# Eight closing stages: the last four k rows of the first 512 columns move next to the second 512 columns, token tile by token tile

## The chip, the cores and the metric

The kernel runs on one core of a Trainium2 chip. The metric is device time in microseconds (us). A core has engines that run their own instruction streams side by side and wait for one another through semaphores: PE (TensorE, matmuls and transposes through the identity matrix), DVE (VectorE), ACT (ScalarE), POOL (GpSimd), and SP, which issues the DMAs here. Each engine takes its instructions in the order in which the build has put them: an instruction that waits holds back everything behind it on its engine.

## What is computed

512 tokens of 1024 features go through four layers. Layer 1 has a state-space mixer (S5 with a GLU), layer 2 a latent attention (MLA), layers 3 and 4 a sparse attention (DSA) beside a gating branch. Each mixer is followed by a feed-forward block. Every one of the eight sub-blocks ends in the same way, and this is all that the change touches:

```python
# y: 512 x K, K = 1024 (out projections) or the last rows of a feed-forward
h = layer_norm(ALPHA * h + y @ w_out, g, b)      # w_out: K x 1024
def layer_norm(x, g, b):
    mu  = mean(x, -1); var = mean(square(x - mu), -1)
    return (x - mu) * rsqrt(var + 1e-5) * g + b
```

Layers 3 and 4 add a gated per-layer embedding, `(p @ w_ple) * sigmoid(x @ w_ple_gate)`, to the feed-forward's sum, and x there is the result of the out projection's LayerNorm.

## The kernel before

Everything is float32. A product is split into three matmuls: the high part `hi` (an ACT cast, L249, in `wpiece`) and the rest `lo` (a subtraction, L109, on DVE or on POOL while the counter `lo_pool`, set to LP = 10, lasts) of the weights, and `xh`, `xl` of the data. `mm3` issues them as L265, L266, L267. A weight piece is two k rows (2 x 128 x 512); raw weights come by SP's DMAs (L242).

**A closing stage.** The eight stages, in the order of time with the moment T (us from the start of the span) at which the last matmul of the stage ends: 1 `ssm_w_out` (328.2), 2 `w_ff2` of layer 1 (673.3), 3 `attn_w_o` (894.7), 4 `w_ff2` of layer 2 (1237.1), 5 `w_o` of layer 3 (1465.6), 6 `w_ffn_out` of layer 3 (1870.0), 7 `w_o` of layer 4 (2097.3), 8 `w_ffn_out` of layer 4 (2515.3). Stages 1, 3, 5, 7 are written in `proj_ln`, stages 2, 4, 6, 8 in `plain`. Tokens lie in four tiles t0 to t3 of 128, each with two PSUM banks: the first 512 columns (nh 0) and the second (nh 1).

`tm_gen` (L280) runs nh 0 weight piece by weight piece over all four token tiles and evacuates the four banks at its end (the residual sum and, later, a LayerNorm statistic; DVE). In stages 3, 5 and 7 these matmuls are fillers of the attention's last units (`proj_first`, L1145). For nh 1 the argument `stagger` is set: all weight pieces are prepared first, then token tile after token tile takes its 24 matmuls (18 in stages 6 and 8), its evacuation and `close` (L422): the rest of the LayerNorm, some 20 DVE instructions, four of them on 128 x 512 elements (L119, two with the mean `mv`, two with the inverse deviation `vy`).

The finished tile is put on `pending`. `flush` (L447) takes one from there and turns it to feature-major with eight transposes on PE (`to_fm`, L127), and the casts and subtractions (`xh` on ACT, `xl` on DVE) that the next stage reads. In `tm_gen` a flush follows a token tile where more than two tiles are pending (L331). So the PE's program has, at the end of a stage: t2's matmuls, to_fm of t0, t3's matmuls, to_fm of t1, then the first matmuls of the next stage, with to_fm of t2 and of t3 among them. Stage 8 has no transposes; it writes the output.

**What sets the order.** A scheduler in the build places all instructions of the program on their engines by an estimate of times, so the order on an engine can differ from the order in which the code is written. What it places doesn't change at run time. Tiles named in the rows carry running numbers.

## Time and profile before

| | before |
|---|---|
| time, median of 3 runs | 2529.29 us (2528.91 to 2530.14) |
| the profiled execution's own time | 2529.88 us |
| span of that execution | 2528.1 us |
| PE busy | 2411.3 us (95%), 11961 matmuls |
| DVE busy | 1559.1 us (62%) |
| ACT busy | 968.8 us (38%) |
| POOL busy | 389.0 us (15%) |
| PE's waits for a LayerNorm's result ahead of a transpose (L127 behind DVE x L119) | 30.8 us in 10 waits |
| mean granted TensorE clock | 0.973 of full speed |

The span counts from the first to the last recorded instruction; 1.8 us of the execution's time lie around it. A timeline row reads: start in us, duration in us, engine, line, operation, output tile <- input tiles, shapes, how many in a row (x), and in brackets the idle time of the engine just before it with the instruction that ended it. The duration of a row "x2" is that of both together. Matmuls overlap, so the pitch of two rows is what one takes.

### The profile page before, as it was taken

What the parts mean: (1) busy time and instruction counts of PE and PEld (TensorE: products, weight loads), DVE (VectorE), ACT (ScalarE), POOL (GpSimd) and SP (SyncE); (2) the same over time, 40 slices, a digit from 0 to 9 for tenths busy, and PEclk for the clock granted to TensorE, in tenths of its full rate; (3) what the DMA queues carried; (4) which work ended last, traced back from release to release, by engine and by line L of the source; (5) the groups of instructions that cost most, each with busy time, mean ns of one, the idle gap of its engine ahead of it and who ended that gap; (6) DMA issues with size and microseconds to landing.
All of it is one profiled execution on the core that took longest, in us unless ns stands there. A gap on an engine that the chain in (4) does not pass through costs nothing.

```text
span 2528.1 us, 30717 instructions
## 1 busy us (share of the span) xinstructions
PE 2411.3 (95%) x11961; PEld 1988.5 (79%) x11961; DVE 1559.1 (62%) x2898; ACT 968.8 (38%) x1563; POOL 389.0 (15%) x378
## 2 busy tenths in 40 slices
PE   7799999999989999999999999999989998999997
PEld 6667888888877888888776878888877687888886
DVE  8744366765666567765695573555569556355655
ACT  4213235445245335444246432333324643223331
POOL 1100110000231220000246220000034622000001
PEclk9779999999999999999999999999999999999999
DMA  4224243322221533222232235232123123423211
GB/s 110 57 57 133 84 150 101 98 88 81 85 71 51 167 92 109 92 92 67 78 127 51 84 121 179 67 133 67 60 86 127 51 86 107 167 67 117 84 59 59
DMA packets 182897, 237.55 MB, mean 94 GB/s; under 512 B 19728, under 2 KB 118816, under 8 KB 182688
## 3 DMA queue, kind: packets, MB, share of 16 engines
q1 hardware_dynamic: 182752, 235.59, 29.5%
q8 instruction: 94, 1.54, 0.3%
q14 instruction: 51, 0.42, 0.1%
HBM read 224.56 MB, written 11.01 MB: 93 GB/s over the span
## 4 chain that ended last, share of the span: by engine, by line
PE 82%; DVE 15%; ACT 2%; DMA 1%; issue 1%; SPq 0%; DVEq 0%; POOL 0%; ACTq 0%
PE ps L265 26%; PE ps L266 25%; PE ps L267 25%; PE ps L127 3%; DVE x L119 2%; PE ps L791 2%; DVE sc L1451 2%; DVE m L1450 2%; DVE x L109 1%; PE ps L789 1%; PE ps L459 1%; DVE vy L109 1%; DVE xl L109 1%; DVE ab L109 1%; DVE sc L119 1%
## 5 line engine op out<-in xcount | busy, mean ns | idle before, releaser
L109 POOL TENSOR_TENSOR wl<-wr,wh 128x1024 fp32r<-128x1024 f32 (+4 forms) x124 | 278.2, 2253 | 1810.9 <-ACT wh L249 1127.0
L249 ACT CAST wh<-wr 128x1024 fp32r<-128x1024 f32 (+4 forms) x300 | 305.7, 1021 | 578.8 <-PE ps L266 287.4
L267 PE MATMUL ps<-xh,wl 128*128 128x512 f32 x1248 | 485.9, 390 | 4.3 <-DVE wl L109 4.3
L265 PE MATMUL ps<-xh,wh 128*128 128x512 f32 x1248 | 486.2, 390 | 0.0
L266 PE MATMUL ps<-xl,wh 128*128 128x512 f32 x1248 | 486.2, 390 | 0.0
L109 DVE TENSOR_TENSOR wl<-wr,wh 128x1024 fp32r<-128x1024 f32 x176 | 217.2, 1236 | 226.5 <-ACT wh L249 225.4
L109 DVE TENSOR_TENSOR wl<-wq,wh 128x1024 fp32r<-128x1024 f32 x140 | 170.5, 1221 | 178.1 <-ACT wh L249 177.7
L267 PEld LDWEIGHTS ps<-xh,wl 128*128 128x128 f32 x1248 | 234.7, 188 | 53.4 <-DVE wl L109 4.7
L265 PE MATMUL ps<-wh,xh 128*128 128x512 f32 (+4 forms) x704 | 270.9, 386 | 4.5 <-DVE rp L109 2.0
L266 PEld LDWEIGHTS ps<-xl,wh 128*128 128x128 f32 x1248 | 234.8, 188 | 48.8
L265 PEld LDWEIGHTS ps<-xh,wh 128*128 128x128 f32 x1248 | 234.6, 188 | 48.6
L266 PE MATMUL ps<-wl,xh 128*128 128x512 f32 (+4 forms) x704 | 263.6, 375 | 0.0
L267 PE MATMUL ps<-wh,xl 128*128 128x512 f32 (+4 forms) x704 | 262.6, 376 | 0.5 <-DVE xl L109 0.5
L249 ACT CAST wh<-wq 128x1024 fp32r<-128x1024 f32 x140 | 147.3, 1052 | 284.1 <-PE ps L266 234.5
L266 PE MATMUL ps<-wl,sh 128*128 128x512 f32 x560 | 217.8, 389 | 0.0
L267 PE MATMUL ps<-wh,sl 128*128 128x512 f32 x560 | 217.5, 389 | 0.0
L265 PE MATMUL ps<-wh,sh 128*128 128x512 f32 x560 | 216.9, 389 | 0.0
L265 PEld LDWEIGHTS ps<-wh,xh 128*128 128x128 f32 x704 | 136.9, 195 | 31.4 <-ACT xh L122 3.5
L267 PEld LDWEIGHTS ps<-wh,xl 128*128 128x128 f32 x704 | 136.1, 194 | 22.1 <-DVE xl L109 1.1
L266 PEld LDWEIGHTS ps<-wl,xh 128*128 128x128 f32 x704 | 137.0, 195 | 18.5
L109 DVE TENSOR_TENSOR x<-x,ps 128x512 f32<-128x512 f32 x156 | 103.0, 681 | 73.4 <-PE ps L267 73.1
L127 PE MATMUL ps<-ident,x 128*128 128x128 f32 x576 | 97.6, 289 | 47.3 <-DVE x L119 30.8
(368 smaller groups left out, 3910.8 us busy)
## 6 DMA issues: line engine op xcount, KB each, us to landing
wr<-in_w_ffn_in_dram SPq DMA_DIRECT2D x44, 1024.0 KB, 5.1
wr<-in_w_ff_dram SPq DMA_DIRECT2D x40, 1024.0 KB, 5.5
wq<-in_w_ff_dram SPq DMA_DIRECT2D x24, 1024.0 KB, 5.1
wq<-in_w_ffn_out_dram SPq DMA_DIRECT2D x16, 1024.0 KB, 8.2
wr<-in_w_in_dram SPq DMA_DIRECT2D x12, 1024.0 KB, 5.5
wr<-in_w_ple_gate_dram SPq DMA_DIRECT2D x8, 1024.0 KB, 5.1
wr<-in_ssm_w_glu_dram SPq DMA_DIRECT2D x6, 1024.0 KB, 5.6
xs<-x SPq DMA_DIRECT2D x24, 256.0 KB, 2.0
```

The source lines that it names most:

```text
L109: (eng or self.nc.vector).tensor_tensor(out, a, b, op)
L119: (eng or self.nc.vector).scalar_tensor_tensor(out, a, s, b, op0, op1)
L127: self.nc.tensor.transpose(out, in_, self.ident[:k, :k])
L249: self.nc.scalar.copy(hi, src)
L265: mm(ps, lh, rh, start=first, stop=False)
L266: mm(ps, lh, rl, start=False, stop=False)
L267: mm(ps, ll, rh, start=False, stop=last)
L459: self.nc.tensor.matmul(bk[:, c], w[:, kt], self.Xh(kt)[:, c], start=kt == 0 and w is hi, stop=False)
L789: nc.tensor.matmul(o, u[:, q * 8 + j, sl], T[:, m * 2 + h, jj], start=True, stop=False)
L791: nc.tensor.matmul(o, H[sl, r, j], ca[sl, r, j].rearrange("p d c -> p (d c)"), start=False, stop=r == 1)
L1450: self.nc.vector.max(m8, s)
L1451: self.nc.vector.match_replace(s, m8, s, -3e38)
```

## The change

The new helpers `begin` and `finish` take the place of both passes. `begin` runs nh 0 with all k rows but the last four, piece by piece over the four token tiles. `finish` prepares the pieces of those last four rows (`p0`) and all pieces of nh 1 (`p1`), and then takes token tile after token tile: 12 matmuls for the rest of nh 0, its evacuation, 24 (18) matmuls of nh 1, its evacuation and `close`. A flush follows where more than one tile is pending, before it was more than two. `p0` gets buffers of its own: in `proj_ln` from a new pool "tail", in `plain` from the tags `sh` and `sl` of the stage's pool. The counter LP = 10 for POOL is set ahead of `p0`. The loads of g and b (`gb`) come later on SP. `proj_first` no longer evacuates, and in stages 5 and 7 no longer splits its pieces over finer steps than `begin` does.

```diff
-    def wpiece(self, src):
+    def wpiece(self, src, spare=None):
         a, b = src.shape[1:]
-        hi = self.tile(self.wp, [P, a, b], F32R, "wh", 5)
-        lo = self.tile(self.wp, [P, a, b], F32R, "wl", 5)
+        if spare is None:
+            hi = self.tile(self.wp, [P, a, b], F32R, "wh", 5)
+            lo = self.tile(self.wp, [P, a, b], F32R, "wl", 5)
+        else:
+            hi, lo = (self.tile(spare, [P, a, b], F32R, tag, 2) for tag in ("sh", "sl"))
...
+    def begin(self, wsrc, xh, xl, order, acc):
+        m = len(order) - 4
+        for pc, ks in self.pieces(wsrc(0), order[:m]):
+            for t in range(NT):
+                if len(acc) <= t:
+                    acc.append(self.bank())
+                self.times(acc[t], t, pc, ks, xh, xl, ks[0] == order[0], False)
+                yield
+
+    def finish(self, wsrc, xh, xl, order, gb, acc, final=None, spare=None):
+        m = len(order) - 4
         gb = self.gb(*gb)
+        if final is None:
+            self.fm_ln()
+        ev0, ev1 = self.residual(False)(0), self.close_ln(gb, 1, False, final)
+        self.lo_pool = LP
+        p0 = list(self.pieces(wsrc(0), order[m:], spare))
+        p1 = list(self.pieces(wsrc(1), order))
+        for t in range(NT):
+            for pc, ks in p0:
+                self.times(acc[t], t, pc, ks, xh, xl, False, ks[-1] == order[-1])
+            ev0(t, acc[t])
+            bk = self.bank()
+            for pc, ks in p1:
+                self.times(bk, t, pc, ks, xh, xl, ks[0] == order[0], ks[-1] == order[-1])
+            ev1(t, bk)
+            if len(self.pending) > 1:
+                self.flush()
...
-        self.fm_ln()
-        for nh in range(2):
-            ev = self.close_ln(gb, nh, True) if nh else self.residual(True)(nh)
-            if nh == 0 and first is not None:
-                for _ in first:
-                    pass
-                continue
-            self.tm(wsrc(nh), list(order), 512, xh, xl, ev, stagger=nh == 1)
...
+        for _ in first:
+            pass
+        if self.X is None:
+            self.unspill()
+        with self.phase("tail") as pool:
+            self.finish(wsrc, xh, xl, order, gb, acc, spare=pool)
```

The lines of the matmuls move by three (L265 to L268 and so on), L249 to L252, L360 to L363. The number and shapes of matmuls, DVE operations and DMAs stay.

Where the instructions stand on PE at the end of stage 5, before. `ps2183` is the bank of nh 1 of t2, `ps2193` that of t3, x2149 and x2150 the two halves of t0, x2151 and x2152 those of t1; `ps2214` belongs to the next stage.

```order
L267 MATMUL ps2183_12085<-wh2165_11981,xl2047_11412 128x512
L127 MATMUL ps2191_12135<-ident2_68,x2149_11944 128x128 x4
L127 MATMUL ps2192_12142<-ident2_68,x2150_11945 128x128 x4
L265 MATMUL ps2193_12149<-wh2158_11966,xh2046_11411 128x512
...
L267 MATMUL ps2193_12149<-wh2165_11981,xl2047_11412 128x512
L127 MATMUL ps2201_12199<-ident2_68,x2151_11946 128x128 x4
L127 MATMUL ps2202_12206<-ident2_68,x2152_11947 128x128 x4
L265 MATMUL ps2214_12236<-wh2205_12218,xh2142_11883 128x512
```

The transposes of t0 stand behind t2's matmuls, those of t1 behind t3's, and the next stage follows.

The same place on PE in the change. `ps2102` is the bank of nh 0 of t3, `ps2185` nh 1 of t2, `ps2195` nh 1 of t3; x2138 and x2139 are t0, x2140 and x2141 t1, x2142 and x2143 t2. Nh 1 of t0 and t1 and the rest of nh 0 of all four tiles stand ahead of the first row.

```order
L270 MATMUL ps2102_11658<-sh2155_11919,xl2047_11420 128x512
L127 MATMUL ps2183_12070<-ident2_68,x2138_11883 128x128 x4
L127 MATMUL ps2184_12077<-ident2_68,x2139_11884 128x128 x4
L268 MATMUL ps2185_12097<-wh2158_11925,xh2046_11419 128x512
...
L127 MATMUL ps2193_12147<-ident2_68,x2140_11885 128x128 x4
L127 MATMUL ps2194_12154<-ident2_68,x2141_11886 128x128 x4
L268 MATMUL ps2195_12174<-wh2158_11925,xh2046_11419 128x512
...
L127 MATMUL ps2203_12224<-ident2_68,x2142_11887 128x128 x4
L127 MATMUL ps2204_12231<-ident2_68,x2143_11888 128x128 x4
L268 MATMUL ps2216_12262<-wh2207_12244,xh2150_11910 128x512
```

Each tile's transposes have moved forward by one token tile: t0's stand directly behind the last matmul of nh 0, t2's directly behind the last matmul of the stage.

DVE at that place in the change: from the evacuation of `ps2102` to the end of t0's LayerNorm.

```order
L119 SCALAR_TENSOR_TENSOR x2144_11889<-x2144_11889,ps2102_11658 128x512
...
L119 SCALAR_TENSOR_TENSOR x2140_11885<-x2140_11885,mv2176_12046,x2146_11902 128x512
L119 SCALAR_TENSOR_TENSOR x2141_11886<-x2141_11886,mv2176_12046,x2147_11904 128x512
L363 BN_STATS st2197_12201<-x2144_11889 128x6
L114 TENSOR_SCALAR rs12180_12054<-ve2178_12051 128x1
L116 TENSOR_SCALAR rt12173_11992<-vy2171_11989,ve2170_11988 128x1
...
L109 TENSOR_TENSOR vy2171_11989<-vy2171_11989,rq12174_11993 128x1
L116 TENSOR_SCALAR rq12182_12056<-rq12182_12056,rt12181_12055 128x1
L119 SCALAR_TENSOR_TENSOR x2138_11883<-x2138_11883,vy2171_11989,x2148_11906 128x512
L119 SCALAR_TENSOR_TENSOR x2139_11884<-x2139_11884,vy2171_11989,x2149_11908 128x512
```

The evacuation of t3 now stands ahead of the last step of t0's LayerNorm, with 21 instructions between the first row and the last two. Stage 7 has the same order with other numbers.

DVE at the end of stage 1 in the change: x296 and x297 are t2, `ps424` is nh 1 of t3, the last matmuls of the stage.

```order
L116 TENSOR_SCALAR rq1421_2481<-rq1421_2481,rt1420_2480 128x1
L119 SCALAR_TENSOR_TENSOR x299_1766<-x299_1766,ps424_2522 128x512
L109 TENSOR_TENSOR vy418_2477<-vy418_2477,rq1421_2481 128x1
L363 BN_STATS st426_2549<-x299_1766 128x6
L119 SCALAR_TENSOR_TENSOR x296_1760<-x296_1760,vy418_2477,x377_2256 128x512
L119 SCALAR_TENSOR_TENSOR x297_1762<-x297_1762,vy418_2477,x378_2258 128x512
```

The last two steps of t2's LayerNorm stand behind the evacuation of t3, and t2's transposes are the ones that now follow the stage's last matmul on PE. Stages 2, 4 and 6 have this order too, stage 6 with more instructions between.

## Rows read from the trace of the kernel before

**Rows 1.** The page: busy time of each engine; shares of the chain that ended last.

```profile
PE 2411.3 (95%) x11961; PEld 1988.5 (79%) x11961; DVE 1559.1 (62%) x2898; ACT 968.8 (38%) x1563; POOL 389.0 (15%) x378
...
PE 82%; DVE 15%; ACT 2%; DMA 1%; issue 1%; SPq 0%; DVEq 0%; POOL 0%; ACTq 0%
```

**Rows 2.** Waits of PE: line waited for: us in total, times, longest.

```profile
PE ps L127 <- DVE x L119: 30.8, 10, 5.5
```

**Rows 3.** Timeline of PE around T in stages 1 to 7 (columns as above).

```profile
327.78 0.39 PE L267 MATMUL ps<-wh,h 128*128 128x512 f32 x1
333.63 1.97 PE L127 MATMUL ps<-ident,x 128*128 128x128 f32 x8 [5.47 <-DVE x L119]
...
676.42 0.90 PE L127 MATMUL ps<-ident,x 128*128 128x128 f32 x3 [3.15 <-DVE x L119]
...
897.52 1.11 PE L127 MATMUL ps<-ident,x 128*128 128x128 f32 x4 [2.10 <-DVE x L119]
...
906.84 0.33 PE L127 MATMUL ps<-ident,x 128*128 128x128 f32 x1 [0.72 <-DVE vy L116]
...
1240.35 0.66 PE L127 MATMUL ps<-ident,x 128*128 128x128 f32 x4 [3.21 <-DVE x L119]
...
1470.35 1.77 PE L127 MATMUL ps<-ident,x 128*128 128x128 f32 x8 [4.71 <-DVE x L119]
...
1864.56 1.32 PE L127 MATMUL ps<-ident,x 128*128 128x128 f32 x8 [1.44 <-DVE x L119]
...
1872.34 0.66 PE L127 MATMUL ps<-ident,x 128*128 128x128 f32 x4 [2.35 <-DVE x L119]
...
2101.98 1.85 PE L127 MATMUL ps<-ident,x 128*128 128x128 f32 x8 [4.71 <-DVE x L119]
...
2106.91 1.54 PE L127 MATMUL ps<-ident,a 128*128 128x128 f32 x6 [2.65 <-DMA a<-in_p_dram]
```

**Rows 4.** Timeline of DVE in stage 1, of POOL in stages 1 and 5.

```profile
328.52 2.22 DVE L109 TENSOR_TENSOR vy<-vy,rq 128x1 f32<-128x1 f32 x1
...
330.78 3.46 DVE L119 SCALAR_TENSOR_TENSOR x<-x,vy,x 128x512 f32<-128x512 f32 x2
...
325.29 7.74 POOL L109 TENSOR_TENSOR wl<-wr,wh 128x1024 fp32r<-128x1024 f32 x3 [16.21 <-ACT wh L249]
...
1462.73 7.02 POOL L109 TENSOR_TENSOR wl<-wr,wh 128x1024 fp32r<-128x1024 f32 x3 [6.64 <-ACT wh L249]
```

**Rows 5.** Timeline of PE and DVE behind the last matmul of stage 8.

```profile
2514.92 0.39 PE L267 MATMUL ps<-wh,wq 128*128 128x512 f32 x1
...
2515.75 0.68 DVE L109 TENSOR_TENSOR x<-x,ps 128x512 f32<-128x512 f32 x1
...
2517.49 1.36 DVE L119 SCALAR_TENSOR_TENSOR x<-x,vy,x 128x512 f32<-128x512 f32 x2
...
2518.89 1.41 DVE L119 SCALAR_TENSOR_TENSOR x<-x,mv,x 128x512 f32<-128x512 f32 x2
...
2520.22 0.15 DVE L109 TENSOR_TENSOR vy<-vy,rt 128x1 f32<-128x1 f32 x1
...
2521.40 1.42 DVE L119 SCALAR_TENSOR_TENSOR x<-x,vy,x 128x512 f32<-128x512 f32 x2
...
2523.67 1.41 DVE L119 SCALAR_TENSOR_TENSOR x<-x,vy,x 128x512 f32<-128x512 f32 x2
```

**Rows 6.** Windows: length, busy time of each engine (instructions), granted clock, DMA share, GB/s.

```profile
1425.00:1446.00 21.00, 21.00 (x124) 17.71 (x123) 10.25 (x24) 8.00 (x19) 5.94 (x12) 1.00 0.68 227
1470.00:1475.00 5.00, 4.65 (x17) 3.79 (x18) 5.00 (x13) 3.40 (x4) 1.23 (x1) 0.66 0.60 210
2105.00:2110.00 5.00, 3.09 (x11) 2.52 (x12) 5.00 (x11) 1.63 (x5) 2.35 (x1) 0.50 0.44 154
```

More of the change, by code (lines that the diff above doesn't have):

```diff
@@ L1030, in plain @@
     def plain(self, pool, n, H, w, row, gb, final):
-        gb = self.gb(*gb)
-        if final is None:
-            self.fm_ln()
         parts = []
@@ L1041, in plain @@
         pick = lambda i: (lambda k: Cols(*(parts[k // n * 2 + t][:, i, k % n] for t in range(2))))
-        for nh in range(2):
-            ev = self.close_ln(gb, nh, False, final) if nh else self.residual(False)(nh)
-            self.tm(self.wslab(w, nh * 512, 512, row), list(range(2 * n)), 512, pick(0), pick(1), ev, stagger=nh == 1)
+        wsrc = lambda nh: self.wslab(w, nh * 512, 512, row)
+        order, acc = list(range(2 * n)), []
+        for _ in self.begin(wsrc, pick(0), pick(1), order, acc):
+            pass
+        self.finish(wsrc, pick(0), pick(1), order, gb, acc, final, pool)
     def strassen(self, pool, n, H, w, row):
@@ L1128, in strassen, with pieces, times @@
         yield
-    def proj_ln(self, wsrc, xh, xl, gb, order=tuple(range(8)), first=None):
-        gb = self.gb(*gb)
+    def pieces(self, wsrc, kts, spare=None):
+        for i in range(0, len(kts), 4):
+            g = kts[i:i + 4]
+            raw = self.wraw(wsrc(g), len(g), 512)
+            for j in range(0, len(g), 2):
+                m = min(2, len(g) - j)
+                yield self.wpiece(raw[:, j:j + m], spare), g[j:j + m]
+    def times(self, bank, t, piece, ks, xh, xl, first, last):
+        hi, lo = piece
+        for i, k in enumerate(ks):
+            self.mm3(bank, xh(k)[:, t * P:(t + 1) * P], xl(k)[:, t * P:(t + 1) * P], hi[:, i], lo[:, i],
+                     first and i == 0, last and i == len(ks) - 1)
@@ L1132, in proj_ln @@
+    def proj_ln(self, wsrc, xh, xl, gb, order=tuple(range(8)), first=None, acc=None):
+        order = list(order)
         if first is None:
             self.new_r()
-        self.fm_ln()
-        for nh in range(2):
-            ev = self.close_ln(gb, nh, True) if nh else self.residual(True)(nh)
-            if nh == 0 and first is not None:
-                for _ in first:
-                    pass
-                continue
-            self.tm(wsrc(nh), list(order), 512, xh, xl, ev, stagger=nh == 1)
@@ L1143, in proj_first @@
-    def proj_first(self, wsrc, xh, xl, order=tuple(range(8)), fine=False):
-        self.new_r()
-        def evac(t, ps):
-            if self.X is None:
-                self.unspill()
-            self.residual(True)(0)(t, ps)
-        return self.tm_gen(wsrc(0), list(order), 512, xh, xl, evac, fine=fine)
+            acc = []
+            first = self.begin(wsrc, xh, xl, order, acc)
+        for _ in first:
+            pass
+        if self.X is None:
+            self.unspill()
+        with self.phase("tail") as pool:
+            self.finish(wsrc, xh, xl, order, gb, acc, spare=pool)
@@ L1153, in rope, with proj_first @@
+    def proj_first(self, wsrc, xh, xl, order=tuple(range(8))):
+        self.new_r()
+        acc = []
+        return self.begin(wsrc, xh, xl, list(order), acc), acc
     def rope(self, dst, src, half, t, c0):
@@ L1406, in mla_ @@
         pick = lambda x: (lambda k: x[:, k])
-        first = self.proj_first(wsrc, pick(oh), pick(ol))
+        first, acc = self.proj_first(wsrc, pick(oh), pick(ol))
         self.attend(units, 2, [(len(units), first)])
-        return lambda: self.proj_ln(wsrc, pick(oh), pick(ol), gb, first=first)
+        return lambda: self.proj_ln(wsrc, pick(oh), pick(ol), gb, first=first, acc=acc)
     def sgu_prep(self, sgu_w, sgu_b):
@@ L1651, in dsa_ @@
             order = list(range(4, 8)) + list(range(4))
-            first = self.proj_first(wsrc, pick("h"), pick("l"), order, True)
+            first, acc = self.proj_first(wsrc, pick("h"), pick("l"), order)
             def some(gen, n):
@@ L1660, in dsa_ @@
                                      (len(units) + 2, first)])
-        return lambda: self.proj_ln(wsrc, pick("h"), pick("l"), gb, order, first=first)
+        return lambda: self.proj_ln(wsrc, pick("h"), pick("l"), gb, order, first=first, acc=acc)
     def swiglu(self, p, w_in, w_out, w_ple, w_pg, gb, final):
```

## The prediction

> **What bounds the kernel now.** I read the page first: PE is busy 95% of the span, and the chain that ended last is PE for 82% and DVE for 15% [rows 1]. So a closing stage costs what PE computes there, which the change leaves alone, plus what PE waits there. Second, PE's waits: the transposes of finished token tiles wait for the LayerNorm's last step in ten places, 30.8 us together [rows 2]. Third, the timeline of PE around T [rows 3]: the largest of these waits begins at T in every stage. In stage 1 the last matmul begins at 327.78, and to_fm of t1 begins at 333.63 after 5.47 us of idle time. The others are 3.15 (stage 2), 2.10 with 0.72 behind it (3), 3.21 (4), 4.71 (5), 1.44 and 2.35 (6), 4.71 (7); stage 7 has 2.65 more for a transfer of p. Fourth, DVE and POOL at that time [rows 4]: POOL subtracts the next stage's lo pieces, 7.74 us in three operations from 325.29, and in these stretches DVE operations that read two SBUF tensors stretch: a `vy` multiplication on 128 x 1 elements takes 2.22 us and a pair of the last LayerNorm step 3.46, where such a pair takes 1.42 and a small operation 0.15 at the end of stage 8 [rows 5]. POOL starts when t3's matmuls free weight buffers, 2.9 us before T in stages 1 and 5 [rows 3, 4], and t3 stays last in the change, so I leave these stretches where they are.
>
> The Trainium skill, GPSIMD Engine Reference, section 1 Specifications, says that POOL and DVE share their SBUF interfaces and contend where a DVE instruction has two SBUF inputs. The rows agree with that; what one such meeting costs, the page doesn't say.
>
> **What the change removes, adds and moves.** PE's matmuls are the same, so is DVE's work. What moves is the place of the transposes. Each tile's to_fm stands one token tile earlier: t0's before t2's nh 1, t1's before t3's, t2's directly at T, with the next stage's first matmuls only behind it. In return a token tile now has 36 matmuls instead of 24, and in this order a LayerNorm has more PE time to hide behind. Whether that is enough is read from the orders on PE and DVE, since a wait that the order forces is there whatever the clock does. One pitch of the small operations: from 2520.22 to 2521.40 DVE did ten in 1.18 us, 0.12 each [rows 5]. A pair of last steps takes 1.4, one alone 0.7, an evacuation 0.68 (0.6 to 0.7 in a row with others) [rows 5].
>
> *Stages 5 and 7, to_fm of t0.* The change says token tile by token tile, but on PE the rest of nh 0 of all four tiles stands together, and to_fm of t0 follows the last of it at once. On DVE the evacuation of that last bank stands ahead of t0's last step. So between these matmuls and to_fm PE must wait for: 0.83 us from the start of a last matmul to the evacuation's start (2514.92 to 2515.75 [rows 5]) less the 0.23 in which the matmul runs anyway, 0.6 for the evacuation, one pair with `mv` 1.4, one statistic 0.6 (an estimate, by the evacuation of the same size), fifteen small operations 1.8, and half of the last pair 0.7: 5.7 us at least. DVE also comes late to that evacuation: in the 5.2 us before it (23 matmuls) it has three evacuations, three or four statistics and a pair, about 6 us. I take 6.8, with 5.7 and 8.5 as ends. A pause like that also lowers the clock: after the 4.71 us of stage 5 the next 5 us ran at 0.66 with 4.65 us of PE busy [rows 6], a loss of 4.65 x 0.34 = 1.6. So each of the two new waits costs 8.4. Nothing covers it: PE's next matmuls stand behind the transposes.
>
> The Trainium skill, TensorE: Matmul & The Clock Gate, Part 1, "What's actually happening", holds that the ramp penalty is under 1% of a typical span and not to be fitted. The rows show it at each of these pauses, and by that rule the sum would be 4.8 us smaller, which lies inside the range.
>
> *Stage 3, to_fm of t0.* The same order with fewer operations between: 3.4 at least, 4.5 taken, with the 1.6 for the clock 6.1.
>
> *Stages 3, 5, 7, the wait at T.* Now t2's result is wanted there. From the end of t2's matmuls to T PE has 24 matmuls at 0.227 and eight transposes, 6.5 us; t2's LayerNorm needs its evacuation, a statistic, two pairs, eight or so small operations and the subtractions of t1's `xl`, 6.4 us uncovered by anything. It would just fit, but its second half meets POOL, as t1's did before: in stage 5 POOL runs until 1469.75 [rows 4], 4.1 after T, and a pair behind that ends 5.5 after T. I take 5.0 in stage 5 (ends 0 and 6) in place of 4.71, 4.0 in stage 3 (0 to 6) in place of 2.82, and no change in stage 7, where PE can't go on before p lands at 2106.91, 9.6 after T [rows 3]. Sums: stage 3 +6.1 + 4.0 - 2.8 = +7.3; stage 5 +8.4 + 5.0 - 4.7 = +8.7; stage 7 +8.4.
>
> *Stages 1, 2, 4, 6.* Here the order on PE is truly tile by tile, and t0 and t1 are in time: 36 matmuls take 8.2 us, a LayerNorm with its evacuation about 6.9. But DVE has the evacuation of t3, which needs T, ahead of t2's last pair. By its operations (0.6 + 0.6 + 0.1 + 0.6 + 0.7 and an interleaved one) to_fm of t2 waits 2.9 us at least; and the pair falls into POOL's stretch, which in stage 1 ends 4.85 after T (325.29 + 7.74 against 328.2 [rows 3, 4]), so that its second half is done near 6.2. Stage 1: 6.2 (2.9 to 7.5) in place of 5.47, +0.7. Stages 2 and 4 have a shorter stretch: 4.6 (3.0 to 5.5) in place of 3.15 and 3.21, +1.4 each. Stage 6 has 17 operations between, 5.3 at least, 6.6 taken, in place of 1.44 + 2.35, +2.8.
>
> *Stage 8.* From T to the end DVE now takes 9.3 us, 2515.75 to 2523.67 + 1.41, with four pairs behind t3's evacuation [rows 5]. In the change three pairs stand there, with the same statistic and fewer small operations: -1.4 for the pair and -0.5 for four of these, -1.9 (-2.5 to 0). What the output's last transfer takes stays.
>
> *The rest.* g and b load later, on SP behind the unspill of x; they are wanted only at the LayerNorm, and the pieces' DMAs stand ahead as before. Two lo pieces per stage change between POOL and DVE, 1.2 us each and beside matmuls. Weight pieces of nh 1 in stages 6 and 8 are ready about when they are wanted: 0, at most 2. In stages 5 and 7, 42 of 48 matmuls that filled the attention's last units, 9.5 us, now come after them. In that stretch PE was busy without a gap, 21.00 of 21.00, and DVE 10.25 and ACT 8.00 [rows 6]; without the filler these units have 11.5 us of PE for 10.25 of DVE, so I take 0, and up to 4 each for the second rival.
>
> Sum: 0.7 + 1.4 + 7.3 + 1.4 + 8.7 + 2.8 + 8.4 - 1.9 = +28.8. Against the profiled execution's 2529.9 that is 2558.7; its own time lies 0.6 above the median, so 2558 us.
>
> **The rivals.** *Waits only move.* At T nothing meets POOL: DVE is ahead since PE gave it 6.8 us in each to_fm of t0, so t2 is done before POOL starts. Then the waits at T fall to what the order forces: stage 1 -2.6, 2 -0.1, 3 +4.5 + 1.6 - 2.8 - 1.6 (one pause for another) = +1.7, 4 -0.2, 5 +6.8 - 4.7 = +2.1, 6 +1.5, 7 +8.4, 8 -1.9: +8.9, 2538 us. For it: DVE's load per tile falls behind PE's 8.2 us. Against it: 6.5 us from t2's evacuation to T for 6.4 us of work.
>
> *Faster.* In stage 7, p lands while PE stands in the new wait ahead of t2: SP's queue reaches it earlier against T, since what holds it, a weight buffer, comes free with t3's first matmuls. If p and t2 are both there at T, the 4.71 + 2.65 us go, with the slow clock behind them (3.09 us busy at 0.50 from 2105, 1.5 us [rows 6]), and stage 7 gives 8.4 - 7.4 - 1.5 = -0.5. With the other stages as in the case above +8.9 - 8.9 = 0, and with to_fm of t0 and the last stage at their best ends (two times -1.1, -1.1 in stage 3, -0.6) -3.9: 2525, and below 2524 where the clock doesn't fall in stages 2 and 4 either. It decides by the transfer: it must land before T + 5. The row that speaks against it is p's release at T + 9.6 with nothing but DMAs ahead.
>
> *Heavier.* The attention's units in stages 5 and 7, without their filler, run at DVE's and ACT's pace: up to 4 us each, and pieces come late in stages 6 and 8, 1 us each: +10, 2568 us. For it: PE would have 11.5 us for what DVE does in 10.25 with semaphores between. Against: no gap shows there now.
>
> *The change doesn't do what it says* is in the forecast already: in stages 3, 5 and 7 the build's order isn't tile by tile.
>
> **How the numbers follow.** Forecast 2558 (its own range 2548 to 2566): 0.60. Waits only move, 2538 (2532 to 2547): 0.15. Heavier, 2568 (2566 to 2576): 0.17. Faster, 2525 (2519 to 2531): 0.08. The range leaves out the fastest case, the lower part of the second and the upper part of the third, some 0.16: 2536 to 2572. A difference of 0.2%, 5.1 us, is about what a measurement of this kernel tells from none. Faster: half of the last case and a little, 0.05. Within: the other half and the lowest end of the second, 0.07. Slower 0.88.
>
> **What would show it.** Right: in PE's waits L127 behind DVE x L119 grows from 30.8 to about 55 us; in stages 5 and 7 a new wait of about 6.8 ahead of t0's transposes, 10 us before T, with the clock down to about 0.7 behind it, and 4.5 in stage 3; the wait at T about 5 in stage 5 and 6 in stage 1; from the last matmul to the end about 1.9 less. Wrong: no gap ahead of t0's transposes in stages 5 and 7 (then t0's last step didn't wait for the evacuation); waits at T under 3 (then DVE met no POOL operation); gaps within the last units of the attention (then the filler was needed).

## The result: 1.6% slower, and where the time went

The changed kernel takes 2568.73 us (median of 4 runs, 2563.3 to 2575.68) where the kernel before takes 2529.72 (2528.91 to 2530.26): a ratio of 1.016, 95% interval 1.0138 to 1.0182, 39 us. The forecast was 2558 in a range of 2536 to 2572. The profiled execution is the slowest of the four, 2575.68 us with a span of 2573.9; its mean granted clock is 0.958, that of the fastest run 0.964.

The page of the changed kernel: busy time, the granted clock in 40 slices, the chain's shares by engine.

```profile
PE 2438.4 (95%) x11961; PEld 2010.4 (78%) x11961; DVE 1562.8 (61%) x2896; ACT 967.1 (38%) x1563; POOL 391.6 (15%) x380
...
PEclk9679999999999999999999999999999898999999
...
PE 83%; DVE 14%; ACT 2%; issue 1%; DMA 0%; POOL 0%; SPq 0%; DVEq 0%; ACTq 0%
```

The number of matmuls is that of [rows 1], and DVE is busy 3.7 us longer. PE is busy 27 us longer for the same matmuls: its clock is lower. PE's longest waits (line waited for: us in total, times, longest):

```profile
PE ps L127 <- DVE x L119: 51.4, 12, 6.5
...
PE ps L127 <- ACT x L1531: 8.9, 2, 7.7
```

The first answers to [rows 2], 30.8 us there. The timeline of PE at the transposes, to be read against [rows 3]:

```profile
334.56 1.86 PE L127 MATMUL ps<-ident,x 128*128 128x128 f32 x8 [4.76 <-DVE x L119]
...
675.91 1.88 PE L127 MATMUL ps<-ident,x 128*128 128x128 f32 x8 [2.85 <-DVE x L119]
...
882.28 0.66 PE L127 MATMUL ps<-ident,x 128*128 128x128 f32 x4 [2.41 <-DVE x L119]
...
900.31 1.97 PE L127 MATMUL ps<-ident,x 128*128 128x128 f32 x8 [4.70 <-DVE x L119]
...
911.10 1.75 PE L127 MATMUL ps<-ident,x 128*128 128x128 f32 x8 [1.94 <-DVE x L119]
...
1245.91 1.85 PE L127 MATMUL ps<-ident,x 128*128 128x128 f32 x8 [2.88 <-DVE x L119]
...
1466.32 1.94 PE L127 MATMUL ps<-ident,x 128*128 128x128 f32 x8 [6.19 <-DVE x L119]
...
1486.27 1.97 PE L127 MATMUL ps<-ident,x 128*128 128x128 f32 x8 [4.68 <-DVE x L119]
...
1891.23 1.97 PE L127 MATMUL ps<-ident,x 128*128 128x128 f32 x8 [6.47 <-DVE x L119]
...
1943.29 0.69 PE L127 MATMUL ps<-ident,x 128*128 128x128 f32 x2 [7.67 <-ACT x L1531]
...
2131.21 1.94 PE L127 MATMUL ps<-ident,x 128*128 128x128 f32 x8 [6.18 <-DVE x L119]
...
2151.50 1.97 PE L127 MATMUL ps<-ident,x 128*128 128x128 f32 x8 [4.68 <-DVE x L119]
...
2156.52 1.51 PE L127 MATMUL ps<-ident,a 128*128 128x128 f32 x6 [2.63 <-DMA a<-in_p_dram]
```

The rows at 1466.32 and 2131.21 are the new waits ahead of t0's transposes in stages 5 and 7, the one at 882.28 that of stage 3. The rows at 334.56, 675.91, 900.31, 1245.91, 1486.27, 1891.23 and 2151.50 stand at T. The row at 911.10 is t3's, behind stage 3. The row at 1943.29 stands in no closing stage: it is the attention of layer 4, where PE waits for the roped keys, the keys with their rotary position embedding (the rope on DVE, then a copy on ACT). The rest of the 51.4 us is one wait of 3.64 at 706.23 in layer 2's attention, which was 3.47 before.

What the wait at 1466.32 is made of stands on DVE: t3's evacuation, a pair with `mv` behind it, and t0's last pair after the small operations.

```profile
1460.99 0.68 DVE L119 SCALAR_TENSOR_TENSOR x<-x,ps 128x512 f32<-128x512 f32 x1
...
1461.71 1.40 DVE L119 SCALAR_TENSOR_TENSOR x<-x,mv,x 128x512 f32<-128x512 f32 x2
...
1465.43 1.41 DVE L119 SCALAR_TENSOR_TENSOR x<-x,vy,x 128x512 f32<-128x512 f32 x2
```

PE's last matmul ahead of these transposes starts at 1459.75, and the transposes start when the first half of that last pair is done.

To see where the span grew I added, over windows of 5 us, PE's idle time and its busy time times (1 - granted clock), for the same stretch of work in both traces. The sum is 169.3 us in the kernel before and 220.7 in the changed one, 51 more where the span is 46 longer, so a stretch's figure is good to about a tenth. The table leaves out the first 250 us (39.4 + 28.1 before, 35.9 + 34.6 changed) and the attention of layer 2 (10.0 + 4.5 and 10.0 + 4.1).

| stretch | before: idle + clock | changed: idle + clock | difference | forecast |
|---|---|---|---|---|
| stage 1 | 5.6 + 1.8 | 4.8 + 1.6 | -1.0 | +0.7 |
| stage 2 | 3.4 + 2.7 | 2.9 + 1.4 | -1.8 | +1.4 |
| stage 3 | 3.2 + 1.1 | 9.2 + 3.7 | +8.6 | +7.3 |
| stage 4 | 3.9 + 1.6 | 4.2 + 1.7 | +0.4 | +1.4 |
| attention of layer 3 | 10.7 + 3.2 | 9.1 + 6.4 | +1.6 | 0 |
| stage 5 | 4.7 + 1.6 | 10.9 + 5.4 | +10.0 | +8.7 |
| stage 6 | 4.5 + 1.4 | 6.5 + 1.7 | +2.3 | +2.8 |
| attention of layer 4 | 10.4 + 3.2 | 17.8 + 19.1 | +23.3 | 0 |
| stage 7 | 7.4 + 3.4 | 13.5 + 6.3 | +9.0 | +8.4 |
| stage 8 and the end | 13.1 + 0 | 11.0 + 0 | -2.1 | -1.9 |

The closing stages together gave +25.4 where +28.8 was forecast. The largest single item is one that the forecast has not at all: the attention of layer 4, a third of it idle time, two thirds a lower clock. The windows there, changed kernel, then kernel before (length, busy time of each engine, granted clock, DMA share, GB/s):

```profile
2010.00:2030.00 20.00, 18.11 (x74) 13.79 (x74) 5.19 (x22) 10.44 (x25) 8.69 (x17) 0.76 0.00 1
2030.00:2050.00 20.00, 19.18 (x95) 14.63 (x94) 8.85 (x34) 12.11 (x29) 9.32 (x12) 0.89 0.17 54
2050.00:2070.00 20.00, 18.99 (x71) 14.91 (x72) 10.01 (x28) 10.94 (x24) 8.33 (x16) 0.57 0.22 52
```

```profile
1995.00:2015.00 20.00, 19.15 (x102) 14.34 (x100) 6.68 (x32) 17.42 (x39) 14.94 (x22) 1.00 0.30 87
2015.00:2035.00 20.00, 19.09 (x111) 14.98 (x111) 15.79 (x46) 13.28 (x33) 8.48 (x15) 1.00 0.10 20
2035.00:2055.00 20.00, 20.00 (x108) 16.08 (x107) 5.61 (x15) 7.34 (x15) 5.71 (x9) 1.00 0.03 3
```

The work there lies 15 to 35 us later in the changed kernel, so the windows don't cover the very same instructions; over these 60 us PE is busy 56.3 us against 58.2, with 240 instructions against 321 and the clock down where it was full.

Part of these 23 us belongs to this one execution. Between the same two matmuls (1890 and 2060 in the kernel before; the clock's changes taken at their own times and not by windows) the kernel before has 10.4 + 3.4 and the changed kernel 17.1 + 19.6. Five kernels of the experiments below have the long wait for roped keys in layer 4 too: e2 16.8 + 9.5, e6 16.9 + 9.5, e7 18.8 + 11.0, e8 19.5 + 10.5, e12 14.1 + 8.1. Of these, e8 is the changed kernel but for one number. Its short waits there are those of the changed kernel (2.23, 1.88 and 1.28 us at 2014.30, 2033.06 and 2059.51), and where the changed kernel's window at 2050 has the clock at 0.57, its own has 1.00:

```profile
2057.60:2077.60 20.00, 17.38 (x102) 13.27 (x101) 13.11 (x36) 12.26 (x28) 10.14 (x19) 1.00 0.24 53
```

So about 12 to 13 us of the 23 come with the kernel (by e2 and e6), and some 10 us with the profiled execution, which is 7 us slower than the median.

### The profile page after: what moved, and what is told of

Its sections match the earlier page's. It is cut to its first block, busy times and chain, and to the rows that moved or that the text cites. A ratio compares the mean times of both kernels' runs of the same rounds, so it can differ in the third digit from the quotient of the medians.

```text
span 2573.9 us, 30737 instructions
## 1 busy us (share of the span) xinstructions
PE 2438.4 (95%) x11961; PEld 2010.4 (78%) x11961; DVE 1562.8 (61%) x2896; ACT 967.1 (38%) x1563; POOL 391.6 (15%) x380
## 4 chain that ended last, share of the span: by engine, by line
PE 83%; DVE 14%; ACT 2%; issue 1%; DMA 0%; POOL 0%; SPq 0%; DVEq 0%; ACTq 0%
PE ps L268 25%; PE ps L269 24%; PE ps L270 24%; PE ps L127 3%; DVE x L119 2%; DVE sc L1493 2%; PE ps L794 2%; DVE m L1492 2%; DVE x L109 1%; PE ps L462 1%; PE ps L792 1%; DVE st L363 1%; DVE sc L119 1%; DVE vy L109 1%; PE ps L695 1%
## 5 line engine op out<-in xcount | busy, mean ns | idle before, releaser
L252 ACT CAST wh<-wr 128x1024 fp32r<-128x1024 f32 (+3 forms) x284 | 288.4, 1019 | 558.1 <-PE ps L269 260.9
L268 PE MATMUL ps<-xh,wh 128*128 128x512 f32 x1248 | 486.5, 390 | 0.0
L109 POOL TENSOR_TENSOR wl<-wr,wh 128x1024 fp32r<-128x1024 f32 (+4 forms) x110 | 242.1, 2213 | 445.5 <-ACT wh L252 445.5
L268 PEld LDWEIGHTS ps<-xh,wh 128*128 128x128 f32 x1248 | 234.8, 188 | 48.9
L268 PE MATMUL ps<-wh,xh 128*128 128x512 f32 (+4 forms) x656 | 255.9, 390 | 2.2 <-DVE rp L109 1.6
L252 ACT CAST wh<-wq 128x1024 fp32r<-128x1024 f32 x140 | 147.4, 1053 | 284.0 <-PE ps L269 234.4
L109 POOL TENSOR_TENSOR sl<-wr,sh 128x1024 fp32r<-128x1024 f32 x16 | 38.7, 2428 | 1410.0 <-ACT sh L252 1410.0
L269 PE MATMUL ps<-wl,xh 128*128 128x512 f32 (+4 forms) x656 | 247.8, 378 | 0.0
L270 PE MATMUL ps<-wh,xl 128*128 128x512 f32 (+4 forms) x656 | 247.5, 377 | 0.0
L268 PE MATMUL ps<-wh,sh 128*128 128x512 f32 x560 | 216.9, 389 | 0.0
L127 PE MATMUL ps<-ident,x 128*128 128x128 f32 x576 | 104.6, 307 | 70.9 <-DVE x L119 51.4
L127 PEld LDWEIGHTS ps<-ident,x 128*128 128x128 f32 x576 | 76.2, 155 | 97.8 <-DVE x L119 42.6
L268 PEld LDWEIGHTS ps<-wh,xh 128*128 128x128 f32 x656 | 129.7, 198 | 25.6 <-issue 2.8
L270 PEld LDWEIGHTS ps<-wh,xl 128*128 128x128 f32 x656 | 128.3, 196 | 20.6 <-issue 0.4
```

Source lines behind the costliest of these rows:

```text
L109: (eng or self.nc.vector).tensor_tensor(out, a, b, op)
L127: self.nc.tensor.transpose(out, in_, self.ident[:k, :k])
L252: self.nc.scalar.copy(hi, src)
L268: mm(ps, lh, rh, start=first, stop=False)
L269: mm(ps, lh, rl, start=False, stop=False)
L270: mm(ps, ll, rh, start=False, stop=last)
```

## Experiments

Theory A: the loss comes from the transposes that stand one token tile earlier, each forced to wait by the orders on PE and DVE. Theory B: from the matmuls that no longer fill the attention of layers 3 and 4. Theory C: from the order in which the build places other work; in the changed kernel 16 top-k rounds of layer 4 (each picks the next eight largest scores) stand on DVE ahead of the first rope operation of the keys, before 11, and PE waits for the roped keys. From the end of the last score's sum to that rope DVE takes 4.2 us before (1912.0 to 1916.2) and 9.7 in the changed kernel (1928.8 to 1938.5): 5.5 us for the five rounds more, where PE's wait is 6.4 longer (7.67 in place of 1.28). All ratios are against the kernel before on the same chip.

**The out projections alone, e1** (stages 1, 3, 5, 7; `plain` as before).

```diff
...
-        for _ in self.begin(wsrc, pick(0), pick(1), order, acc):
-            pass
-        self.finish(wsrc, pick(0), pick(1), order, gb, acc, final, pool)
+        for nh in range(2):
+            ev = self.close_ln(gb, nh, False, final) if nh else self.residual(False)(nh)
+            self.tm(self.wslab(w, nh * 512, 512, row), list(range(2 * n)), 512, pick(0), pick(1), ev, stagger=nh == 1)
```

> The change in the out projections alone (stages 1, 3, 5, 7); stages 2, 4, 6, 8 as before. Theory A, the waits ahead of t0's transposes: gaps of about 2.4 us in stage 3 and 6.2 us in stages 5 and 7 as in the changed kernel, each with about 1.6 us of slow clock behind it, 0.7 less in stage 1, the waits at T of 4.7 in stages 3, 5, 7: about +23 us, 2552. Theory B, the attention of the sparse layers lost the matmuls that filled it: on top of that the clock is low (0.6 to 0.8) for some 50 us in the attention of layer 4 where it was full before, 10 to 15 us more, 2562 to 2567. Theory C, the order of the top-k rounds in layer 4, which in this kernel is that of before (11 rounds ahead of the first rope operation, in the changed kernel 16): if that is what slows the attention of layer 4, the low clock is gone here.

Measured: 2552.35 us (2551.97 to 2553.07), ratio 1.0087 (1.0072 to 1.0101). Theory A's number. Theory B falls: the filler is gone here as in the changed kernel, and layer 4's attention costs 10.0 + 4.8 us against 10.4 + 3.4 before, with the clock at 0.85 in one window and full in the next two. What the units without filler show is small: in the changed kernel PE waits 0.29 and 0.68 us in the last units of either attention (1431.66 and 1436.63, 2096.56 and 2101.51).

```profile
1990.00:2010.00 20.00, 20.00 (x88) 15.52 (x89) 8.73 (x46) 14.08 (x35) 15.24 (x22) 0.85 0.01 1
2010.00:2030.00 20.00, 19.17 (x101) 14.24 (x99) 7.16 (x34) 15.55 (x38) 10.20 (x19) 1.00 0.16 53
2030.00:2050.00 20.00, 20.00 (x122) 15.68 (x120) 16.20 (x47) 16.06 (x36) 13.23 (x19) 1.00 0.24 53
```

**The feed-forwards alone, e2** (stages 2, 4, 6, 8; `proj_ln` as before).

```diff
-        with self.phase("tail") as pool:
-            self.finish(wsrc, xh, xl, order, gb, acc, spare=pool)
...
+            self.tm(wsrc(nh), list(order), 512, xh, xl, ev, stagger=nh == 1)
...
```

> The change in the feed-forwards alone (stages 2, 4, 6, 8); stages 1, 3, 5, 7 as before. By the changed kernel's gaps: stage 2 -0.3, stage 4 -0.3, stage 6 +2.7 with some clock, stage 8 -1.4: about +2 us, 2532, were that all. The build also places 16 instead of 11 top-k rounds ahead of the first rope operation of layer 4 here. Theory C: that gives PE's wait of 7.7 us for the roped keys in place of 1.3, and slow clock behind it, about +10 us more, 2540 to 2542. Theory B (filler matmuls): they are there in this kernel, so the attention of layer 4 runs at full clock and the time is at most 2540.

Measured: 2541.76 us (2540.99 to 2543.47), ratio 1.0046 (1.0033 to 1.0059), as theory C has it. The wait for roped keys is there (7.53 us at 1929.18) and the clock is at 0.76 from 1995 to 2015 though the filler is present. The two halves together give +34 of the change's +39; the rest is within the 12 us over which the changed kernel's runs scatter.

**Stages 2, 4 and 8 alone, e5, and stage 6 alone, e6.** `plain` uses the new code for some calls only.

```diff
+        if final is not None or n == 4:      # in the other kernel: final is None and n == 3
+            return self.plain_new(pool, n, H, w, row, gb, final)
...
```

> The change in stages 2, 4 and 8 alone; stage 6 and the out projections as before. The build places 11 top-k rounds ahead of the first rope in both sparse layers, as before. Theory C (in the feed-forwards only stage 6 costs, by its own wait and by the order of the top-k rounds it brings): no wait over 2 us for roped keys, stages 2 and 4 -0.3 each, stage 8 -1.4, so 2527, under both kernels. If stages 2 and 4 cost something that the gaps don't show, 2530 or more.

> The change in stage 6 alone, with 16 top-k rounds ahead of the first rope in layer 4. Theory C: a wait of 6.5 us at T of stage 6 in place of 1.4 and 2.3, a wait of 7.5 us for roped keys in place of 1.3, and slow clock behind them for 40 us: +2.7 + 6.2 + 3 to 5 = +12 to 14, 2542 to 2544. If the loss in layer 4 comes from several stages together, under 2537.

Measured: 2524.26 us (2522.17 to 2532.59, 11 runs), ratio 0.9982 (0.9973 to 0.999), for the first; 2544.4 us (2543.48 to 2544.96), 1.0055 (1.0042 to 1.0069), for the second. So all that the feed-forwards lose, they lose in stage 6, and most of it behind the stage: 2.4 us of the 14.5 lie at the stage and 12.6 in layer 4's attention. The timeline of PE with stage 6 alone shows the wait at T and the wait for roped keys.

```profile
1876.47 1.97 PE L127 MATMUL ps<-ident,x 128*128 128x128 f32 x8 [6.48 <-DVE x L119]
...
1929.01 0.69 PE L127 MATMUL ps<-ident,x 128*128 128x128 f32 x2 [7.65 <-ACT x L1554]
```

In the first kernel no wait for roped keys in layer 4 reaches 1 us. Its gain is 3 us more than the gaps at T and the end account for. By its trace that lies in layer 4's attention: 6.8 us idle in place of 10.4 at the same loss of clock, with no wait for roped keys over 0.4 us in place of 1.28 and a wait for POOL of 0.46 in place of 2.96. Layer 3's attention is the same in sum (12.0 + 1.7 against 10.7 + 3.4).

**Stage 8 alone, e4.**

```diff
+        if final is not None:
+            return self.plain_new(pool, n, H, w, row, gb, final)
...
```

> The kernel before with the change in stage 8 alone. From the last matmul on DVE has one pair of LayerNorm steps less: from the start of the last evacuation to the end of the last step 7.9 us in place of 9.3, everything ahead as before: -1.4 us, 2528. If the tail is bound by the output's transfers instead, 2529.3.

Measured: 2527.83 us (2515.72 to 2531.27, 12 runs), ratio 0.9988 (0.9978 to 0.9998). The gain is of the size forecast, at the edge of what these runs tell. The rows in the changed kernel, against [rows 5]:

```profile
2562.97 0.69 DVE L109 TENSOR_TENSOR x<-x,ps 128x512 f32<-128x512 f32 x1 [0.49 <-PE ps L270]
...
2564.78 1.40 DVE L119 SCALAR_TENSOR_TENSOR x<-x,mv,x 128x512 f32<-128x512 f32 x2
...
2566.53 1.41 DVE L119 SCALAR_TENSOR_TENSOR x<-x,vy,x 128x512 f32<-128x512 f32 x2
...
2569.49 1.41 DVE L119 SCALAR_TENSOR_TENSOR x<-x,vy,x 128x512 f32<-128x512 f32 x2
```

Three pairs behind the last evacuation in place of four, 7.93 us to the end of the last in place of 9.33; this run's own trace has 7.94.

**The rest of the first columns in the usual ring, e3** (out projections; nothing in the attention's memory).

```diff
-        with self.phase("tail") as pool:
-            self.finish(wsrc, xh, xl, order, gb, acc, spare=pool)
+        self.finish(wsrc, xh, xl, order, gb, acc)
...
+        if spare is None:
+            pc, ks = p0.pop(0)
+            for t in range(NT):
+                self.times(acc[t], t, pc, ks, xh, xl, False, False)
```

> The changed kernel, but in the out projections the rest of the first columns is one piece (two k rows) in the usual ring of five buffers instead of two pieces in the pool that takes the attention's memory: nothing waits for the attention's buffers, the filler matmuls are back in the attention, and on DVE t0's LayerNorm ends ahead of the evacuation of t3's first columns. Theory A: the gaps of 6.2 us ahead of t0's transposes in stages 5 and 7 fall under 1 us, the waits at T stay near 4.7 in stages 5 and 7; in layer 3 the build places 16 top-k rounds ahead of the first rope here and 11 in layer 4, so a wait of 5 to 8 us moves to layer 3. 2529.3 + 2 (feed-forwards) + 2 to 4 (stage 3, 5, 7) + about 8 = about 2542. If DVE's load alone, and not the forced order, makes the gaps, they stay near 6 and the time near 2560.

Measured: 2564.43 us (2559.66 to 2567.51), ratio 1.0133 (1.0119 to 1.0147), not 2542. Part of the mechanism showed: in stage 5 the transposes of t0 don't wait, nothing waits at T there, and the wait for roped keys moved to layer 3 with the order of the rounds. In stage 7 t0's transposes still wait 1.36 and 2.19 us in two parts, not under 1. And forced waits came up elsewhere, 4.48 us ahead of t0's transposes in stage 1, 4.58 in stage 3, 3.26 ahead of t1's in stage 5.

```profile
894.71 1.94 PE L127 MATMUL ps<-ident,x 128*128 128x128 f32 x8 [4.58 <-DVE x L119]
...
1311.74 0.69 PE L127 MATMUL ps<-ident,x 128*128 128x128 f32 x2 [7.67 <-ACT x L1534]
...
1491.11 1.11 PE L127 MATMUL ps<-ident,x 128*128 128x128 f32 x4 [3.26 <-DVE x L119]
```

So another order moved the waits to other tiles and did not remove them. What of this is the pool's place in memory and what the shorter tile is not shown: with one piece of rest a tile has 30 matmuls here, not 36. I had read the orders of stages 5 and 7 alone when I gave the number.

**POOL's share, e8** (changed kernel with LP = 6).

```diff
-LP = 10
+LP = 6
```

> The changed kernel with LP = 6: POOL subtracts the closing stage's own six lo pieces and none of the next stage's, which fall to DVE. Theory A's second part, POOL's subtractions hold DVE's last LayerNorm steps at T: with POOL idle there the waits at T fall from 4.7 to about 3 in stage 1 and under 2 in stages 3 and 5, while DVE has three more operations of 1.25 us at the start of each stage; gaps ahead of t0's transposes unchanged at 6.2. 8 to 12 us of gaps less, 2558. If DVE's own queue makes the waits, they grow by up to 3.7 each and the time is over 2575.

Measured: 2586.33 us (2581.71 to 2588.68), ratio 1.0225 (1.0209 to 1.024): not theory A's fall, but the growth that the expectation names as the rival, DVE's own queue. First DVE and POOL at T of stage 5 in the changed kernel:

```profile
1475.27 0.69 DVE L119 SCALAR_TENSOR_TENSOR x<-x,ps 128x512 f32<-128x512 f32 x1 [6.90 <-PE ps L270]
...
1479.22 1.86 DVE L109 TENSOR_TENSOR vy<-vy,rt 128x1 f32<-128x1 f32 x1
...
1481.86 1.52 DVE L109 TENSOR_TENSOR vy<-vy,rq 128x1 f32<-128x1 f32 x1
...
1483.42 3.46 DVE L119 SCALAR_TENSOR_TENSOR x<-x,vy,x 128x512 f32<-128x512 f32 x2
...
1478.65 7.01 POOL L109 TENSOR_TENSOR wl<-wr,wh 128x1024 fp32r<-128x1024 f32 x3 [29.21 <-ACT wh L252]
```

DVE is idle for 6.90 us ahead of t2's evacuation, so nothing is late there but t2 itself, and three of its operations take 1.7, 1.4 and 2.0 us longer while POOL subtracts than such operations do elsewhere (0.15, 0.15 and 1.41). With LP = 6 POOL is idle at that point, and the pair has its usual length again, but it ends later:

```profile
1481.97 1.23 DVE L109 TENSOR_TENSOR wl<-wr,wh 128x1024 fp32r<-128x1024 f32 x1
...
1483.35 1.23 DVE L109 TENSOR_TENSOR wl<-wr,wh 128x1024 fp32r<-128x1024 f32 x1
...
1484.71 1.23 DVE L109 TENSOR_TENSOR wl<-wr,wh 128x1024 fp32r<-128x1024 f32 x1
...
1486.51 1.28 DVE L109 TENSOR_TENSOR xl<-ps,xh 128x512 fp32r<-128x512 f32 x2
...
1492.88 1.41 DVE L119 SCALAR_TENSOR_TENSOR x<-x,vy,x 128x512 f32<-128x512 f32 x2
```

The waits at T are 8.85, 9.00 and 8.74 us in stages 1, 3 and 5, where the pieces went to DVE ahead of t2's last steps, and 8.80 in stage 7, 4.1 to 4.3 more than in the changed kernel (three subtractions of 1.23 are 3.7), and unchanged in stages 2, 4 and 6 (2.86, 2.87, 6.48). While POOL subtracts, steps of DVE that PE waits for take longer; what the wait would be with the subtractions on neither engine is not shown, since here they went to DVE.

**The number in the flush, both ways.** The changed kernel with a later flush, e7, and the kernel before with the earlier one, e12.

```diff
-            if len(self.pending) > 1:        # changed kernel
+            if len(self.pending) > 2:
```

```diff
-                if not by_token and len(self.pending) > 2:   # kernel before
+                if not by_token and len(self.pending) > 1:
```

> The changed kernel with one number as before: a flush where more than two tiles are pending. So t1's transposes, not t2's, stand at T; those of t0 still stand behind the last matmul of the rest of the first columns in stages 5 and 7 (17 top-k rounds ahead of the first rope in layer 4). Theory A: the gaps of 6.2 us ahead of t0's transposes stay in stages 5 and 7, and the waits at T (4.8, 2.9, 4.7, 2.9, 4.7, 6.5 in stages 1 to 6) fall to under 1.5 us each, with the clock behind them: 20 to 25 us of gaps and 5 to 8 of clock less, about 2540. If the waits at T come from POOL holding DVE whichever tile is wanted, they stay and the time stays near 2565.

> The kernel before with one number of the change: a flush where more than one tile is pending; its tiles stay at 24 matmuls. The build places 16 top-k rounds ahead of the first rope in layer 4. Theory A: the transposes one tile earlier are the loss, with or without the longer tiles: t0's stand behind t1's matmuls, 5.4 us after t0's own, for a LayerNorm of 7 us and more: 2 to 5 us in each of seven stages, and at T t2's wait 5 to 9 in place of 3 to 5: 30 to 50 us, with 10 for layer 4: 2570 to 2590. If the change's order of the matmuls is the loss, about 2540.

Measured: 2530.49 us (2526.34 to 2536.86, 10 runs), ratio 1.0006 (0.9997 to 1.0016), for the changed kernel with the later flush: 38 us gone with one number, 10 more than expected. And 2575.12 us (2574.22 to 2578.72), ratio 1.0197 (1.0168 to 1.0225), for the kernel before with the earlier flush: 45 us lost with it, as expected. Some 8 of the 45 lie in layer 4's attention (14.1 + 8.1 against 10.4 + 3.4), where the build's order changed too. PE's waits for the LayerNorm are 14.4 us with the later flush and 59.3 with the earlier one alone:

```profile
PE ps L127 <- DVE x L119: 14.4, 6, 3.7
```

```profile
PE ps L127 <- DVE x L119: 59.3, 18, 6.3
```

With the later flush no wait for the LayerNorm is left at T; behind T, ahead of t2's transposes, 1.63 us are left in stage 1 and 1.16 and 0.60 in stage 3. In stage 7 PE then waits 8.07 us for the transfer of p, in place of 2.63. The wait for roped keys stays (7.93 us, 17 rounds). The gaps ahead of t0's transposes in stages 5 and 7 did not stay at 6.2, as I had written, but fell to 3.66: t2's matmuls of nh 1 now stand ahead of them.

**Later flush where the order is good.** The new code with the later flush in stages 1, 2, 4, 6 and 8, the out projections of the attentions as before (e9, first edit); and the same with a high priority on the rope (e10, second edit).

```diff
-            if len(self.pending) > 1:
+            if len(self.pending) > 2:
...
-        return lambda: self.proj_ln(wsrc, pick("h"), pick("l"), gb, order, first=first, acc=acc)
+        return lambda: self.proj_ln_old(wsrc, pick("h"), pick("l"), gb, order, first=first)
...
```

```diff
-            self.rope(y3[:, :, 0:16], p3[:, :, 0:16], 8, t, 32)
+            with self.tc.high_priority():
+                self.rope(y3[:, :, 0:16], p3[:, :, 0:16], 8, t, 32)
```

> The change with a flush only where more than two tiles are pending, in stages 1, 2, 4, 6 and 8; stages 3, 5 and 7 as before (no pool in the attention's memory). The build places 17 top-k rounds ahead of the first rope in layer 4. Theory A (the tiles of 36 matmuls are no loss, the transposes one tile earlier are): waits at T fall from 5.5 to 1.6 in stage 1 and to nothing in 2, 4 and 6, with the clock behind them, stage 8 -1.4: about -21; theory C: +10 to 12 for the wait for roped keys and the clock behind it: 2520. If the longer tiles cost something by themselves, 2530 or more.

> The kernel of e9_late_flush with one difference: the four DVE operations of the rope in the sparse layers get a high priority in the build, which then places 11 top-k rounds ahead of the first rope in layer 4, as before the change. Theory C: the wait of 7.5 us for roped keys falls to under 2 and the clock stays full behind it: 10 to 12 us less than e9_late_flush, about 2509. If the order of the top-k rounds only moves the waits, the two agree within 3 us.

The third kernel, e11, has the two edits that stand above for the ring and for the later flush.

> The kernel of e3_rest_in_ring (all eight stages, the rest of the first columns in the usual ring in stages 1, 3, 5, 7) with a flush only where more than two tiles are pending; 11 top-k rounds ahead of the first rope in both sparse layers. Theory A: no forced wait ahead of t0's transposes and none at T but for p in stage 7: gaps of L127 behind DVE under 12 us in all, 2505 to 2515, under e3_rest_in_ring by 50. If the pieces in the ring come too late, gaps ahead of the rest of the first columns and 2520 or more.

Measured: 2514.1 us (2511.29 to 2518.31, 9 runs), ratio 0.9949 (0.9936 to 0.9963), for the first, and 2512.55 us (2509.21 to 2515.16, 7 runs), ratio 0.9939 (0.992 to 0.9958), for the second: both beat the kernel before and the changed one. The number of rounds in the first expectation was misread: that kernel has 11 rounds ahead of the rope, not 17, so the two programs hardly differ and say nothing on theory C. Without theory C's term the first expectation comes to about 2509, and the measured time lies 5 over that. Its trace has the stages as expected (the five that are new lose 23 us less than before), and more loss of clock outside them, in the first 250 us and in the attentions of layers 3 and 4 (36.8, 8.1 and 6.8 us against 28.8, 3.4 and 3.4); why is open. The kernel with the ring and the later flush in all stages takes 2523.61 us (2503.4 to 2526.19, 10 runs), ratio 0.9971 (0.9948 to 0.9994), not 2505 to 2515, and PE's waits for the LayerNorm are 27.6 us, not under 12: in stages 1, 3, 5 and 7 t1's transposes wait 5.7 to 6.0 us at T, where a tile has 30 matmuls, the rest being one piece. In the kernel of e9 stages 3, 5 and 7 wait as before the change, stage 1 hardly, 2, 4 and 6 not at all:

```profile
334.27 0.41 PE L127 MATMUL ps<-ident,x 128*128 128x128 f32 x2 [1.63 <-DVE x L119]
...
1905.74 0.44 PE L127 MATMUL ps<-ident,x 128*128 128x128 f32 x2 [1.75 <-ACT x L1554]
...
2089.26 1.97 PE L127 MATMUL ps<-ident,x 128*128 128x128 f32 x8 [4.71 <-DVE x L119]
```

**What stands behind theory C.** Over the kernels the wait for the roped keys follows the order: 16 or 17 rounds ahead of the rope in the changed kernel, in e2, e6, e7, e8 and, in layer 3, in e3, with waits of 7.5 to 7.9 us (5.61 in e12, also 16); 11 rounds in layer 4 of the kernel before, e1, e4, e5, e9, e10 and e11, with at most 1.8, and in layer 3 of all kernels but e3, with at most 2.4. A kernel in which nothing but this order differs was not tried.

## Why the prediction was right, and where it was short

*The kind of loss was right.* The waits were read from the program's orders, and they came where they were placed: 6.19 and 6.18 us ahead of t0's transposes in stages 5 and 7 (forecast 6.8), 4.70, 4.68 and 4.68 at T of stages 3, 5 and 7 (4.0, 5.0, no change), 6.47 at T of stage 6 (6.6), 1.8 us less from the start of the last matmul to the end of the span (1.9 less). PE's waits for L119 grew to 51.4 us (forecast 55). That the stages' sum is so near, +25.4 for +28.8, is in part misses that cancel: stages 3, 5 and 7 came to +27.6 (forecast +24.4), stages 1, 2 and 4 to -2.4 (+3.5).

*Small misses.* Stage 3's wait ahead of t0's transposes is 2.41 and 0.19 us, under the 3.4 that I had called the least, and 1.94 us ahead of t3's at 911.10 stood in no term. In stage 6 the order on PE is not tile by tile, as I had read it: the 24 matmuls of t2's and t3's rest stand together ahead of t0's transposes (from 1868.81), so t2's LayerNorm has 18 matmuls and eight transposes to hide behind and not 30 matmuls; the price came from DVE's order and fitted. Stages 2 and 4 wait 2.85 and 2.88 instead of 4.6, which is the 2.9 that the order forces: POOL's subtractions end at 674.45 (669.86 + 4.59) and 1244.50 (1239.85 + 4.65), ahead of t2's last pair at 675.13 and 1245.13. Stage 1 waits 4.76 instead of 6.2; POOL's three operations there take 7.02 us where they took 7.74 [rows 4], and the pair behind them 2.96.

```profile
326.94 7.02 POOL L109 TENSOR_TENSOR wl<-wr,wh 128x1024 fp32r<-128x1024 f32 x3 [28.00 <-ACT wh L252]
...
332.21 2.96 DVE L119 SCALAR_TENSOR_TENSOR x<-x,vy,x 128x512 f32<-128x512 f32 x2
```

In stage 5 the slow clock behind the new wait cost more than the 1.6 us taken: the two windows there hold 3.68 us busy at 0.50 and 5.00 at 0.86, 2.5 us.

```profile
1465.00:1470.00 5.00, 3.68 (x13) 3.32 (x14) 3.33 (x10) 0.00 (x0) 0.00 (x0) 0.50 0.00 0
1470.00:1475.00 5.00, 5.00 (x20) 4.06 (x20) 0.00 (x0) 0.00 (x0) 0.00 (x0) 0.86 0.00 0
```

*The term that was missing.* The measured time lies 10.7 us over the forecast. The sum had nothing for the attention of layer 4, where 23 us went in the profiled execution and 12 to 13 in the kernels of e2 and e6; that is about the whole miss. I had followed the order on PE and DVE at the closing stages and not behind stage 6, where it shows the five more top-k rounds ahead of the rope. The rival called heavier had a price of about that size, 10 us, and with it the range reached up to 2572; but its reason was wrong: the filler's absence costs next to nothing (e1), and the loss is there with the filler present (e2, e6). That the measured time lies in the range is in part luck.

*What decided.* The change carries two things: longer tiles (36 matmuls a tile) and an earlier flush. The prediction counted them together. Apart, the flush alone costs 45 us (e12), and taking it back returns 38 (e7); with it taken back, the longer tiles gain 15 us in stages 1, 2, 4, 6 and 8 (e9), of which stage 8, without transposes, has about 2.

## What to carry to other kernels

Where a step is put at an engine's queue head, ask not only whether its input's engine has the capacity but how long the chain from the last input to the step is, against the work that stands between: here one token tile of distance (5 to 8 us of PE's work from t2's last matmul to T) was too little for a chain of 7 us with a wait in the order. Two tiles of 36 matmuls were enough: no wait at T in stages 1, 2, 4 and 6, and 1.63 us behind it in stage 1 (e9); two of 24 or of 30 were not (5.47 and 5.72 us in stage 1, kernel before and e11). Before costing a change to a program whose order a scheduler sets, compare the orders of the whole program and not only of the lines that the diff touches. Try a change's parts apart: one of these two was worth 15 us, where it was kept, and the other cost 45.
